# Layer two: three steps of neighbourhood attention placed between the output gate's projection tiles

## The chip, the cores and the metric

One core of a Trainium2 chip runs the kernel; the other cores are idle. The metric is the device time of one execution in microseconds, the median of several runs. The engines are named as in the profile: PE (TensorE, matrix products), DVE (VectorE), ACT (ScalarE), POOL (GpSimd), SP (SyncE, which here issues the DMAs).

## The reference, cut to what matters

A two-layer diffusion backbone over 512 latent tokens (a grid of 8 rows by 64 columns) and 256 context tokens, width 1024, all in float32. Each layer normalises and modulates its input, multiplies it by one wide input matrix, and splits the result into three groups of heads:

```
q_c, kv_c, k_pe, nq, nk, nv, dn = split_in(h @ w_in[l])
mla_o = multi-head latent attention (4 heads, up-projections, softmax over context + latent)
na_o  = neighbourhood attention     (4 heads of 64; 16 columns around each query, plus context)
dn_o  = gated DeltaNet              (4 heads of 128, two directions, chunks; output gate silu(z))
x = x + gate * (concat(mla_o, na_o, dn_o) @ w_out[l])
x = x + gate * swiglu(...)
```

In layer two the context stream is no longer updated, so only the 512 latent tokens are queries there. The three groups of heads don't depend on one another until the output projection. `z`, the DeltaNet's output gate, is one of the slices of the input projection: 512 columns, four tiles of 128.

## The kernel before

Every matrix product on the large weights is done in three passes: weight and activation are each split into a rounded part (`h`) and a remainder (`l`), and `gemm` adds hh, hl and lh. A weight tile is loaded by SP (`wr`), rounded by ACT (`wh`, line 216), and its remainder taken by POOL (`wl`, line 217; a few on DVE).

The code writes one program order per engine, mostly by hand; a planner (the tile framework's scheduler, with a simulated timeline) then fixes the issue order of each engine before the run, and may issue an instruction ahead of earlier ones if its buffers are free. On the chip each engine issues in that fixed order.

The part of a layer that matters here, in program order:

1. *Projections* of keys, values and queries of DeltaNet, with their convolutions; then those of neighbourhood attention (`do_nk`, `do_nq`, `do_nav`). On the side DVE inverts 32x32 blocks (`base_inverse`).
2. *Tail* (lines 979 to 990). `inverse(0, ...)` builds the 128x128 inverses of two chunks from the blocks. Then a string of letters, one for each layer, gives the order of what is left: `k` is `do_kv` (latent keys and values, with a normalisation), `q` is `do_ql` (the two query tiles of latent attention), `z` is `do_z` (the next of four gate tiles: projection into one of two PSUM banks of 512 columns, tanh on ACT at line 794, product on DVE at line 795, store). When the tail is over, the projections' buffers and PSUM banks are released; the DeltaNet's working buffers are claimed on their place.
3. *Neighbourhood attention beside DeltaNet* (lines 1109 to 1112). `attention()` is a generator; each `next(na)` is one step: one of four blocks of 128 queries for one pair of heads, so eight steps in layer two. A step does, for each of two heads, scores on PE (`s_na`, twelve small matmuls for both heads, two PSUM banks), row maxima with the bias added on DVE (lines 870 to 876), two exponentials on ACT (877, 878), the denominator and the scaling on DVE (882 to 884), four transposes on PE (`tp_na`, line 889) and a copy of them (`pt`, line 891, ACT for the first head and DVE for the second); then sixteen small matmuls with the values (`o_na`) and a copy. Only the last step of a pair issues a DMA.
   Before each step `beside` takes as many items from the DeltaNet list `dn` as the list `DNS` says. The items are scans of one chunk in one direction (`scan(d, x)`: state times keys `ks`, product with the inverse `yp`, state update `sp`, and where there is output `qs` and `oa`), the second and third `inverse`, and a release of banks.
4. *Latent attention* (lines 1119 to 1233), with the rest of the list, and then the output projection, which needs all three.

A scan can only start when the DeltaNet's buffers are there, that is after the last gate tile. The second `inverse` begins with four mask products on POOL (line 945) and transposes on DVE.

```
for i in TAIL[l]:
    tail[i]()
...
def beside(ada, sb):
    for _ in range(next(dn_n, 16)):
        next(dn, lambda: 0)()
...
while True:
    beside(ada, sn)
    if next(na, None) is None:
        break
```

Of the kernel before, what the change touches and what calls it, by code (L numbers as in the profile page):

```python
# [34 lines left out]
BN = dict(S=2, T=3)  # L35
BM = dict(S=3, T=3)
ADA = ([2] * 12, [])
DNS = ([1, 0, 0] + [1] * 4 + [0] + [1] * 12, [0, 0, 2, 1, 1, 2, 1, 1, 2, 3] + [2] * 11)
ADA_T = "T"
EB = dict(e=5)  # L40
BO = {512: 3, 256: 2}
# [1 line left out]
PRE0, LATE = True, ()  # L43
ROW = lambda S, V: S.copy
HLP = ([(k, 1) for k in range(8)], [], [(k, 1) for k in (0, 2, 4, 6, 7)], [])
TAIL = ["zzzzkq", "kzzqzz"]
INV = ((4, 3), (4, 3))
WV = ((6,), (23,))
MR = 2
# [313 lines left out]
def layer(tc, nc, a, l, es_x, xT, env, nx):  # L363
# [426 lines left out]
    def do_z(h):  # L790
        n = nT
        th, z = ctmp("thz"), ctmp2("z")
        for cols, acc in proj(TILE_Z + h, need_ctx):
            tanh = S.activation(out=th[:, cols], in_=acc, func=AF.Tanh, scale=0.5)
            stt(out=z[:, cols], in0=th[:, cols], scalar=1.0, in1=acc, op0=ALU.add, op1=ALU.mult)
        if h == 3:
            e.preload(tanh)
        nc.sync.dma_start(out=d_z[:, 0:n // P, h], in_=z[:, :n].rearrange("p (c d) -> p c d", d=P))
# [44 lines left out]
    def open_na():  # L843
        nonlocal sn
        sn = pool(es_w, f"sb_na{l}", side=B_)
# [135 lines left out]
    inverse(0, sb_i, att_bank)  # L981
    if "n" in TAIL[l]:
        open_na()
    z = iter(range(4))
    tail = dict(k=do_kv, q=do_ql, z=lambda: do_z(next(z)), n=lambda: next(na))
    for i in TAIL[l]:
        tail[i]()
    es_i.close()
    es_h.close()
    es_p.close()  # L990
    if "n" not in TAIL[l]:
        open_na()
# [80 lines left out]
    def finish(c, tok, o):  # L1073
# [13 lines left out]
        for h in range(4):  # L1087
# [6 lines left out]
               S_(0, 4), S_(1, 5), S_(0, 5), S_(1, 4), S_(0, 3), S_(1, 2)])  # L1094
    dn_n, ada_n = iter(DNS[l]), iter(range(3 * KD))

# [370 lines left out]
```

## Time and profile before

| | us |
|---|---|
| median of 3 runs | 2146.63 |
| the three runs | 2128.88, 2146.63, 2149.4 |
| the profiled execution, its own time | 2147.42 |
| its span in the profile | 2145.6 |
| PE busy | 2008.8 (94%) |
| DVE busy | 1176.9 (55%) |
| ACT busy | 714.1 (33%) |
| POOL busy | 758.7 (35%) |

The profile is of one execution. Times in it count from the start of its span. The clock that was granted to PE is given as a share of full speed; it has two levels, 1.2 and 2.4 GHz, so 0.50 means that all of a stretch ran at the lower one. A busy PE is not PE at its peak, since its matmuls overlap. Idle time of an engine is put down to what ended it.

### The profile page before, as it was taken

The page shows a single profiled execution, that of the slowest core. Times are in us where ns is not written, and L with a number is a line of the kernel's source. Part 1 is how long each engine was busy: PE and PEld are TensorE (multiplying, and loading weights), DVE is VectorE, ACT ScalarE, POOL GpSimd, SP SyncE. Part 2 cuts the span into 40 slices and gives each one's busy share as a digit, 9 for nine tenths or more (in the row PEclk, how much of TensorE's full clock was granted, in tenths as well). Part 3 has the DMA queues.
Part 4 walks back from the last instruction along what each step waited for, and adds up shares of the span by engine and source line. Part 5 has one row for each costly group of instructions (what it writes and reads, how often), then busy time and mean ns, then how long its engine had stood idle before and what let it go on. Part 6 is the DMA issues. An engine that isn't in the chain of part 4 may idle for free. (4 is left out here: it accounts for less than half of the span.)

```text
span 2145.6 us, 32031 instructions
## 1 busy us (share of the span) xinstructions
PE 2008.8 (94%) x12770; PEld 1699.3 (79%) x12770; DVE 1176.9 (55%) x2045; ACT 714.1 (33%) x1385; POOL 758.7 (35%) x540
## 2 busy tenths in 40 slices
PE   6899998998998999999999998889899889999998
PEld 4788787887787888888888876777688678888887
DVE  4888814768656447347343458882559654222123
ACT  5333323335444121121122344324334443222233
POOL 3465233113323222232323445623202252444444
PEclk9999998999999999999999999999679999999999
DMA  7324253542322435244342512424222232332332
GB/s 278 80 79 147 80 157 100 176 155 77 102 71 79 130 118 164 92 130 158 107 128 70 155 34 71 151 73 134 74 67 87 67 105 67 93 95 94 102 96 91
DMA packets 119309, 232.56 MB, mean 108 GB/s; under 512 B 30516, under 2 KB 55988, under 8 KB 119032
## 3 DMA queue, kind: packets, MB, share of 16 engines
q1 hardware_dynamic: 119160, 230.51, 34.2%
q8 instruction: 101, 1.65, 0.3%
q14 instruction: 48, 0.39, 0.1%
HBM read 199.46 MB, written 31.01 MB: 107 GB/s over the span
## 5 line engine op out<-in xcount | busy, mean ns | idle before, releaser
L217 POOL TENSOR_TENSOR wl<-wr,wh 128x1024 fp32r<-128x1024 f32 (+2 forms) x188 | 440.4, 2343 | 829.3 <-ACT wh L216 810.8
L216 ACT CAST wh<-wr 128x1024 fp32r<-128x1024 f32 (+2 forms) x190 | 193.5, 1019 | 717.9 <-PE acc_gu L104 289.2
L104 PE MATMUL acc_gu<-fh,wh 128*128 128x512 f32 (+1 forms) x1024 | 358.8, 353 | 9.6 <-ACT fh L304 8.7
L104 PE MATMUL acc_gu<-fl,wh 128*128 128x512 f32 (+1 forms) x1024 | 360.7, 353 | 4.1 <-DVE fl L305 4.1
L104 PE MATMUL acc_gu<-fh,wl 128*128 128x512 f32 (+1 forms) x1024 | 359.9, 352 | 0.0
L104 PE MATMUL acc_in<-hh,wh 128*128 128x512 f32 (+1 forms) x640 | 229.0, 362 | 16.9 <-ACT xp L491 6.2
L104 PE MATMUL acc_in<-hl,wh 128*128 128x512 f32 (+1 forms) x640 | 228.6, 358 | 3.0 <-DVE hl L305 2.0
L104 PE MATMUL acc_in<-hh,wl 128*128 128x512 f32 (+1 forms) x640 | 225.3, 356 | 2.1 <-POOL wl L217 2.0
L104 PEld LDWEIGHTS acc_gu<-fh,wh 128*128 128x128 f32 x1024 | 194.0, 190 | 37.2 <-ACT fh L304 11.0
L1348 DVE TENSOR_TENSOR av<-acc_gu,av 128x768 f32<-128x768 f32 (+1 forms) x44 | 36.3, 825 | 337.7 <-PE acc_gu L104 329.7
L104 PEld LDWEIGHTS acc_gu<-fl,wh 128*128 128x128 f32 x1024 | 195.0, 190 | 30.5 <-DVE fl L305 4.3
L104 PEld LDWEIGHTS acc_gu<-fh,wl 128*128 128x128 f32 x1024 | 194.8, 190 | 26.2
L104 PEld LDWEIGHTS acc_in<-hh,wh 128*128 128x128 f32 x640 | 125.1, 196 | 43.3 <-issue 8.1
L104 PE MATMUL acc_d<-al,wh 128*128 128x512 f32 (+1 forms) x444 | 157.2, 354 | 0.0
L104 PE MATMUL acc_d<-ah,wh 128*128 128x512 f32 (+1 forms) x444 | 157.2, 354 | 0.0
L104 PE MATMUL acc_d<-ah,wl 128*128 128x512 f32 (+1 forms) x444 | 156.1, 354 | 0.0
L254 DVE CUSTOM_DVE_ANT_0 junk<-wada,scb 128x1024 f32<-128x1024 f32 x112 | 144.1, 1286 | 7.9 <-DMA wada<-w_adaT 5.2
L104 PEld LDWEIGHTS acc_in<-hl,wh 128*128 128x128 f32 x640 | 125.7, 196 | 24.8 <-DVE hl L305 4.6
L104 PEld LDWEIGHTS acc_in<-hh,wl 128*128 128x128 f32 x640 | 124.8, 196 | 21.1 <-POOL wl L217 3.4
L1366 DVE SCALAR_TENSOR_TENSOR xT<-acc_d,mod,xT 128x512 f32<-128x512 f32 (+1 forms) x76 | 46.5, 634 | 155.4 <-PE acc_d L104 155.4
L501 DVE SCALAR_TENSOR_TENSOR cy<-xp,cw,cy 128x770 f32<-128x770 f32 (+1 forms) x96 | 118.9, 1239 | 22.5 <-ACT cy L499 20.4
L1352 DVE TENSOR_TENSOR al<-av,ah 128x768 fp32r<-128x768 f32 (+1 forms) x44 | 100.4, 2282 | 35.1 <-ACT ah L1351 35.1
(390 smaller groups left out, 3906.2 us busy)
## 6 DMA issues: line engine op xcount, KB each, us to landing
wr<-w_gu SPq DMA_DIRECT2D x88, 512.0 KB, 3.5
wada<-w_adaT SPq DMA_DIRECT2D x56, 512.0 KB, 3.3
wr<-w_in SPq DMA_DIRECT2D x48, 512.0 KB, 3.5
wr<-w_dn SPq DMA_DIRECT2D x32, 448.0 KB, 3.3
wada<-w_ada SPq DMA_DIRECT2D x24, 512.0 KB, 3.4
wada<-w_ada SPq DMA_DIRECT2D x8, 1024.0 KB, 8.3
wr<-w_dn SPq DMA_DIRECT2D x16, 512.0 KB, 3.5
xT<-xT SPq DMA_DIRECT2D x16, 384.0 KB, 5.3
```

Of the source, the lines that this page charges most:

```text
L104: nc.tensor.matmul(out, lhsT, rhs, start=start, stop=stop)
L216: S.copy(out=hi[:, sl], in_=raw[:, sl])
L217: eng.tensor_tensor(out=lo[:, sl], in0=raw[:, sl], in1=hi[:, sl].bitcast(F32), op=ALU.subtract)
L254: V.tensor_tensor_reduce(out=junk, in0=w, in1=scb[:, s], scale=1.0, scalar=0.0, op0=ALU.mult, op1=ALU.add, accum_out=mod[l][:, part, j, s: ...
L501: stt(out=y[:, :wid], in0=xp[:, j:j + wid], scalar=w_(j), in1=y[:, :wid], op0=ALU.mult, op1=ALU.add)
L1348: tt(out=av[:, :nT], in0=accs[1][:, :nT], in1=av[:, :nT], op=ALU.mult)
L1352: after.append(tt(out=l_[:, :nT], in0=av[:, :nT], in1=h_[:, :nT].bitcast(F32), op=ALU.subtract))
L1366: stt(out=xT[:, m, st_], in0=acc, scalar=mod[l][:, 5, m, s:s + 1], in1=xT[:, m, st_], op0=ALU.mult, op1=ALU.add)
```

## The change

Layer two's tail gets the letter `n`, one step of neighbourhood attention, three times, and its order is changed; layer two's list of DeltaNet items for each step is shortened by the three steps that are gone from the later loop (the buffers of the steps are then claimed before the tail instead of behind it).

```
-DNS = ([1, 0, 0] + [1] * 4 + [0] + [1] * 12, [0, 0, 2, 1, 1, 2, 1, 1, 2, 3] + [2] * 11)
+DNS = ([1, 0, 0] + [1] * 4 + [0] + [1] * 12, [2, 2, 2, 1, 1, 2, 3] + [2] * 11)
...
-TAIL = ["zzzzkq", "kzzqzz"]
+TAIL = ["zzzzkq", "kznqznznz"]
```

Before, layer two's order is k, z, z, q, z, z and then eight steps with 0, 0, 2, 1, 1, 2, 1, 1 items ahead of them and 2 behind the last. After, it is k, z, step 0, q, z, step 1, z, step 2, z and then five steps with 2, 2, 2, 1, 1 items ahead of them and 2 behind the last. In both, 10 items of the list are done when the loop ends. Line 982 opens the steps' buffers ahead of the tail when the string has an `n`.

## Rows read from the trace of the kernel before

**Rows 1.** The page, part 2: granted clock of PE in 40 equal slices

```profile
PEclk9999998999999999999999999999679999999999
```

**Rows 2.** Windows of layer two: span, busy time (instructions) by engine, clock, DMA

```profile
1443.00:1507.00 64.00, 58.54 (x440) 47.35 (x439) 15.83 (x37) 26.87 (x45) 22.45 (x12) 0.95 0.44 126
1507.00:1526.70 19.70, 9.92 (x101) 8.21 (x99) 17.34 (x32) 6.56 (x17) 12.15 (x8) 0.83 0.41 135
1526.70:1578.00 51.30, 51.30 (x342) 43.58 (x338) 21.98 (x66) 13.48 (x45) 3.12 (x3) 0.50 0.13 42
1578.00:1608.00 30.00, 30.00 (x403) 26.13 (x403) 19.89 (x50) 10.52 (x32) 2.69 (x4) 1.00 0.21 66
1624.00:1668.00 44.00, 39.36 (x320) 33.96 (x320) 40.06 (x92) 20.80 (x68) 11.04 (x15) 1.00 0.23 68
```

The five engines stand in the order PE, weight loads of PE, DVE, ACT, POOL.

**Rows 3.** Timeline of PE behind the last gate tile: start, duration, what, [idle before]

```profile
1510.31 1.09 PE L104 MATMUL o_na<-pt,nav 128*64 128x128 f32 x16 [2.34 <-ACT pt L891]
...
1515.40 0.63 PE L889 MATMUL tp_na<-cst,pr 128*128 128x128 f32 x4 [2.21 <-DVE pr L884]
1520.09 1.12 PE L889 MATMUL tp_na<-cst,pr 128*128 128x128 f32 x4 [4.07 <-DVE pr L884]
1521.00 1.92 PE L104 MATMUL yp<-vp,Y 128*128 128x128 f32 x8
```

**Rows 4.** Timeline of DVE: the add early and late, and a scaling

```profile
1515.18 2.30 DVE L882 TENSOR_TENSOR st<-st 128x1 f32<-128x1 f32 x1
...
1540.59 0.16 DVE L882 TENSOR_TENSOR st<-st 128x1 f32<-128x1 f32 x1 [1.59 <-ACT pr L878]
...
1543.23 0.49 DVE L884 TENSOR_SCALAR pr<-pr,st 128x512 f32<-128x512 f32 x1
```

**Rows 5.** Groups of DVE from 1507 to 1608: busy us, mean ns | idle before

```profile
L884 DVE TENSOR_SCALAR pr<-pr,st 128x512 f32<-128x512 f32 x14 | 12.0, 857 | 0.4
...
L882 DVE TENSOR_TENSOR st<-st 128x1 f32<-128x1 f32 x14 | 5.5, 395 | 3.6 <-ACT pr L878 3.4
```

**Rows 6.** Timeline of POOL: mask products of the second inverse

```profile
1510.30 9.45 POOL L945 TENSOR_TENSOR Y<-strips,cst 128x1024 f32<-128x1024 f32 x4
```

**Rows 7.** Windows of 2 us, where the clock falls

```profile
1466.00:1468.00 2.00, 2.00 (x8) 1.58 (x8) 1.38 (x4) 0.99 (x2) 1.66 (x1) 0.50 0.92 309
...
1516.00:1518.00 2.00, 0.03 (x1) 0.00 (x0) 1.93 (x3) 0.59 (x1) 2.00 (x2) 0.62 0.61 224
...
1526.00:1528.00 2.00, 2.00 (x21) 1.77 (x17) 1.42 (x5) 2.00 (x9) 0.00 (x0) 0.68 0.04 8
```

**Rows 8.** Timeline of PE: one group of state updates at either clock

```profile
1542.60 2.07 PE L104 MATMUL sp<-w,kt 128*128 128x128 f32 x8
...
1585.84 1.16 PE L104 MATMUL sp<-w,kt 128*128 128x128 f32 x8
```

**Rows 9.** The chain that ended last: start, duration, what

```profile
1573.31 2.00 PE ks L104 x8
1575.31 1.71 PE qs L104 x8
...
1585.00 0.91 PE s_na L104 x6
...
1597.72 0.59 PE tp_na L889 x4
```

**Rows 10.** Timeline of PE: gaps in the tail

```profile
1461.57 0.50 PE L104 MATMUL acc_in<-hh,wh 128*128 128x512 f32 x1 [1.62 <-ACT wh L216]
...
1465.38 0.58 PE L104 MATMUL s_na<-nkh,nqh 64*128 64x256 f32 x1 [1.88 <-ACT pr L878]
```

**Rows 11.** Timeline of ACT: the first gate tile's tanh among exponentials

```profile
1462.49 1.28 ACT L794 ACT_TABLE_LOAD   x1
1463.79 0.60 ACT L794 ACTIVATE thz<-acc_in 128x512 f32<-128x512 f32 x1
1464.28 0.50 ACT L877 ACTIVATE pr<-pr,st 128x256 f32<-128x256 f32 x1
```

## The prediction

> **What bounds the kernel now.** I read the page first: TensorE (PE) is busy 94% of the span, and the row of granted clocks [rows 1] is 9 almost everywhere but for one dip, "67", in the slices from 1502 to 1609 us. That is layer two's neighbourhood attention, the stage that the change touches. So I cut this part into stretches [rows 2]. In the tail stage (1443 to 1507: key/value tile, four gate tiles, query tiles, first block inverse) PE is busy 58.54 of 64 us at a clock of 0.95. Then 1507 to 1526.7: PE busy 9.92 of 19.70, VectorE (DVE) 17.34. Then 1526.7 to 1578: PE busy all 51.30 us, but at 0.50 of its clock. Then 1578 to 1608: PE again busy throughout, at 1.00. The chain of waits agrees: it runs over DVE in the second stretch and over PE in the third and fourth.
>
> Two losses stand there. The first is idle PE after the last gate tile. The next transposes of probabilities wait for the softmax: 2.34, 2.21 and 4.07 us [rows 3], 9.8 of the 19.70 us in all [rows 2]. Two reasons show. The first two attention steps have nothing beside them (zero DeltaNet items each), so one softmax chain is all there is to do; and DVE is slow just then: a one-column add takes 2.30 us where another takes 0.16 [rows 4], and fourteen scalings, 0.49 each when nothing hinders, take 12.0 [rows 4, 5], beside GpSimd's four mask products for the second inverse, 9.45 us from 1510.30 [rows 6]. The second loss follows from the first: the granted clock falls to its lower level at 1516 to 1518 (mean 0.62 there), right in the longest gap, comes back once (0.83 is the mean of the whole stretch), falls again at 1526 to 1528 (0.68) [rows 7], and stays at 0.50 until 1578 [rows 2]. At 0.5 the same eight matmuls take 2.07 us instead of 1.16 [rows 8]; the 51.30 us would be about 25.7 at full clock.
>
> The Trainium skill (TensorE: Matmul & The Clock Gate, HAM oscillation) says that gaps between bursts of matmuls throttle the array, and that sustained activity releases it. The trace agrees with the first half: the fall sits in the 4.07 us gap. It does not bear out the second as far as busy time goes: 51.30 of 51.30 us busy left the clock at 0.50.
>
> **The change part by part.** *What moves.* Steps 0 to 2 of eight go ahead of the second, third and fourth gate tile (step 0 behind the first one and before the query tiles). Of the DeltaNet list, the ten items that stood before the stage's end still stand there; from step 4 on the order is the same as before. What changes is that the first two scans now come before step 3 instead of step 2, and nothing of the steps 0, 1 and 2 stands between the last gate tile and them. Layer one is untouched.
>
> *TensorE.* A step at full clock is two score groups of 0.91 us, two groups of transposes of 0.59 [rows 9] and the values' product of 1.09 [rows 3]: 4.1 us. Scores already run ahead as far as two score banks let them (step 0's before 1443, step 1's in the tail), so what enters the tail is three steps' transposes and products, 6.8 us, step 2's scores and, running ahead in turn, step 3's, 3.6 us: some 10.5. They leave the stage behind. The work is not less; what can be won is idle time and clock.
>
> *Tail.* Now it loses 5.5 us idle [rows 2], of which 1.62 and 1.88 stand where step 0 will be ready [rows 10], and about 3 us from a half-clock piece around 1466 [rows 7] behind those gaps. Bounds: 6.5 us won if the step fills them, 0 if the planner leaves them, and a loss if new gaps come (the rival below); I take 3 won, half of it.
>
> *ScalarE.* Tanh of the gates and exponentials of the softmax now alternate. After the table load for tanh at 1462.49 an exponential runs at 1464.28 with none between [rows 11], so I cost alternation at nothing. The cover for the rest is the slack: ScalarE is busy 26.87 and DVE 15.83 of the tail's 64 us [rows 2]; all of DVE's work from 1507 to 1608 is 59 us (the three stretches of [rows 2]) with eight steps and ten DeltaNet items in it, so three steps bring well under a third, some 14 us as an estimate, which fits. Were that slack gone, the gate's evacuation would be late and hold one of the two projection banks.
>
> *Queues.* Steps 0 to 2 issue no DMA (the output goes out after step 3 of a pair) and nothing on GpSimd, so neither SP's nor GpSimd's queue gets anything; the weights' loads keep their order. On PE the steps are queued past the projections, on ScalarE past their weight casts.
>
> *After the last gate tile.* The loads of the first scan start when that tile's buffers are free, but its product runs only at 1521.00 [rows 3], behind both transposes of step 1. With the scans first it can run 4 to 5 us after the tile, and step 3's softmax can be ready by then, as step 0's was. So of the 9.8 us idle I leave 3: 6.8 won. Bounds: 9.8, and 0 if the mask products starve DVE in the same way, which the trace cannot exclude: they still start there.
>
> *Clock.* From 1507 to 1608 PE has about 8 + 25.7 + 30 = 64 us of full-clock work, 53.5 after the move. If the clock holds, 25.7 us and some 1.6 of the short dip are won. I leave one short dip, 3.3 us: 24. But then DVE binds more. Its work until 1578 is 17.3 + 22.0 us, some 8.4 of it excess of the slow instructions (12.0 - 14 x 0.49 for the scalings, 5.5 - 14 x 0.16 for the adds [rows 4, 5]); less that and some 9.5 for what leaves (the 14 without what already ran ahead), 21.5 against 23 us of PE work. The nearest stretch with both so loaded is 1624 to 1668: DVE 40.06 of 44, PE 39.36, that is 89%, at clock 1.00 [rows 2]. By it 53.5 us of work take 60.1: 6.6 lost. If only the first 23 us suffer it is 3; I take 6.6, since the mask products come on top.
>
> **Sum:** 3 + 6.8 + 24 - 6.6 = 27 us won. The profiled execution took 2147.42 us (span 2145.6 and 1.8 around it), 0.8 over the median of the three runs, 2146.63: so about **2120 us**. The three runs reach from 2128.88 to 2149.4; one 18 us faster would fit a clock that came back earlier, but no trace shows it.
>
> **The rivals.** *The clock falls again and stays.* For it: GpSimd's 9.45 us of masks follow the last gate tile in any order, and DVE instructions with operands in SBUF stall beside them [rows 4, 6]; once low, the clock stayed low over 51 us of mixed small matmuls. Against: denser work right there. In the trace it rose with the first pair of state products that stand side by side (2.00 and 1.71 us from 1573.31 [rows 9]), those of the scan that follows the second inverse; of the changed order some 23 us of full-clock work lie ahead of that, 46 at half instead of the 32 that I allow. Gain 27 - 14: 2134 us. The Trainium skill (SBUF — State Buffer, Who interferes with whom) speaks for this: GpSimd and a DVE instruction with two SBUF operands exclude each other on a shared port, and the later one waits in full. The 2.30 us add agrees with it.
>
> *Nothing is given back.* The planner reorders across steps already (step 1's scores run in the tail), so the issue order may hardly change, or the idle time moves to the scans' chain of matrix product, scaling and state update. Then 2147, give or take 5.
>
> *Slower: the steps stop the projections.* ScalarE and DVE issue in order. If a copy of transposed probabilities is queued ahead of a gate tile's tanh, and its transpose stands on PE behind a projection, the tile's bank stays held and PE waits out the softmax. Price: the waits of a bare step, 2.34 + 2.21 us or up to 4.07 + 2.34 [rows 3], times three, 14 to 19 us, with the low clock later as now: some 2162 us. It decides where such a wait in the tail is over about 3 us a step with no gain behind. Against it: the tail's slack and the two banks.
>
> **How the numbers follow.** Held clock 0.50 (2110 to 2130), low clock again 0.27 (2128 to 2143), nothing 0.11 (2142 to 2152), slower 0.12 (2155 to 2170). 1% is about what a measurement of this kernel can tell from no change; it is 21.5 us, a bound at 2125. Faster: three quarters of the first case and a tenth of the second, 0.40. Slower: 0.13. Within 1%: 0.47. The range: from 2106 (all idle time and no DVE loss) to 2147, which holds the first two cases and half of the third.
>
> **What would show it.** Right: in the profile after, exponentials and transposes of steps 0 to 2 between the gate tiles; the first scan's product within some 5 us of the last gate tile; the clock row without the "67"; the stage after the gate tiles about 60 us instead of 101. The tail longer by about 8 us, not 20. Wrong: a fall of the clock within 10 us of the last gate tile that lasts over 20; gaps of PE over 2 us between gate tiles that end with a transposed copy or a gate's evacuation; or a later stage that takes back what this one wins, since latent attention behind it is the DVE-loaded stretch.

## The result and the profile after

The changed kernel takes 2121.74 us, the median of 7 runs (2119.09 to 2125.45); the kernel before, run beside it, 2147.81 us (7 runs). The ratio is 0.9889, 95% interval 0.986 to 0.9917: 26 us, a little over 1%. The runs of the kernel before spread over the whole study from 2128 to 2162 us, and their mean granted clock goes with the time: at 2128 to 2135 us it is 0.965 to 0.971, near 2147 us 0.958 to 0.962, from 2159 us up 0.952 to 0.955.

The profiled execution of the changed kernel took 2125.45 us (span 2123.6). Its page, part 2, the granted clock in 40 equal slices; the "67" of [rows 1] is gone:

```profile
PEclk9999998999999999999999999999999999999999
```

Windows of the changed kernel, to set beside [rows 2]: the tail; from the end of the last gate tile to the fall of the clock; the low piece; the rest of neighbourhood attention.

```profile
1448.00:1519.30 71.30, 65.62 (x487) 52.30 (x485) 23.81 (x65) 32.52 (x65) 22.65 (x12) 0.93 0.41 116
1519.30:1532.30 13.00, 8.86 (x115) 7.34 (x114) 10.81 (x22) 5.46 (x14) 11.79 (x8) 1.00 0.58 193
1532.30:1539.10 6.80, 6.62 (x45) 6.11 (x45) 2.95 (x12) 2.24 (x6) 1.04 (x1) 0.50 0.14 39
1539.10:1583.70 44.60, 44.60 (x606) 38.87 (x605) 29.71 (x83) 16.60 (x52) 4.94 (x6) 1.00 0.27 75
```

The stage behind the gate tiles is 64.4 us long (1519.3 to 1583.7) where it was 99.2 (1507.0 to the end of the last `o_na` at 1606.2). 6.8 us of it run at half clock; before it was 58.0, in windows of 1 us from 1516.5 to 1523.3 and from 1526.7 to 1577.9. From 1539.1 on PE does not wait at all, with DVE busy 29.71 of 44.60 us.

The timeline of PE in the changed kernel, against [rows 3]:

```profile
1504.19 1.09 PE L889 MATMUL tp_na<-cst,pr 128*128 128x128 f32 x8
...
1510.41 1.09 PE L104 MATMUL o_na<-pt,nav 128*64 128x128 f32 x16
1511.44 0.66 PE L889 MATMUL tp_na<-cst,pr 128*128 128x128 f32 x4
...
1518.93 0.39 PE L104 MATMUL acc_in<-hh,wl 128*128 128x512 f32 x1
1519.25 1.09 PE L104 MATMUL o_na<-pt,nav 128*64 128x128 f32 x14
...
1525.39 0.38 PE L104 MATMUL s_na<-nkh,nqh 64*128 64x256 f32 x1 [1.51 <-ACT pr L878]
...
1526.30 1.16 PE L104 MATMUL yp<-vp,Y 128*128 128x128 f32 x8
...
1532.48 2.08 PE L104 MATMUL sp<-w,kt 128*128 128x128 f32 x8 [2.81 <-DVE w L1035]
...
1535.49 1.97 PE L889 MATMUL tp_na<-cst,pr 128*128 128x128 f32 x8
1537.25 1.91 PE L104 MATMUL yp<-vp,Y 128*128 128x128 f32 x8
```

Step 0 from its transposes on, the transposes of step 1 and the scores of step 2 stand between the gate tiles; step 1's last fourteen products and step 2 from its transposes on run behind the last one. The three waits for softmax of [rows 3] are gone. What is left is 1.51 and 2.81 us. The second wait is the old mechanism at a new victim, as DVE and GpSimd show (timelines of the changed kernel):

```profile
1507.65 0.48 DVE L884 TENSOR_SCALAR pr<-pr,st 128x512 f32<-128x512 f32 x1
...
1515.69 0.48 DVE L884 TENSOR_SCALAR pr<-pr,st 128x512 f32<-128x512 f32 x1
...
1527.91 1.62 DVE L882 TENSOR_TENSOR st<-st 128x1 f32<-128x1 f32 x1
1529.45 0.41 DVE L870 TENSOR_REDUCE st<-s_na 128x1 f32<-128x256 f32 x1
1529.78 2.04 DVE L882 TENSOR_TENSOR st<-st 128x1 f32<-128x1 f32 x1
1531.75 0.68 DVE L1035 TENSOR_TENSOR w<-yp,scal 128x512 f32<-128x512 f32 x1
```

```profile
1522.54 9.27 POOL L945 TENSOR_TENSOR Y<-strips,cst 128x1024 f32<-128x1024 f32 x4
```

The scalings of steps 0 and 1 now run before GpSimd's mask products, at 0.48 us. In the kernel before, those of step 1 stood beside them (timeline of DVE there; two more of the slow instructions behind [rows 5]):

```profile
1512.91 2.35 DVE L884 TENSOR_SCALAR pr<-pr,st 128x512 f32<-128x512 f32 x1
...
1517.71 2.33 DVE L884 TENSOR_SCALAR pr<-pr,st 128x512 f32<-128x512 f32 x1
```

In the changed kernel the scalings have escaped. Two adds still fall beside the mask products (1.62 and 2.04 us), and this time the scaling `w` of the first scan is queued behind. Between the two adds the row maximum, which reads PSUM, takes its usual 0.41 us. The groups of DVE from 1519.3 to 1583.7 say what is left of [rows 5]: the scalings cost nothing extra any more, the adds some 3.3 us.

```profile
L882 DVE TENSOR_TENSOR st<-st 128x1 f32<-128x1 f32 x10 | 4.9, 490 | 0.2
L884 DVE TENSOR_SCALAR pr<-pr,st 128x512 f32<-128x512 f32 x10 | 4.9, 498 | 0.1
```

The gaps of the tail [rows 10] stayed as they were, 1.70 for 1.62 and 1.87 for 1.88 us:

```profile
1467.03 0.50 PE L104 MATMUL acc_in<-hh,wh 128*128 128x512 f32 x1 [1.70 <-ACT wh L216]
...
1470.83 0.58 PE L104 MATMUL s_na<-nkh,nqh 64*128 64x256 f32 x1 [1.87 <-ACT pr L878]
```

### The profile page after: what moved, and what is told of

Same layout as the page of the kernel before. It is cut to its first block, busy times and chain, and to the rows that moved or that the text cites. A ratio compares the mean times of both kernels' runs of the same rounds, so it can differ in the third digit from the quotient of the medians.

```text
span 2123.6 us, 32023 instructions
## 1 busy us (share of the span) xinstructions
PE 1990.2 (94%) x12770; PEld 1684.4 (79%) x12770; DVE 1172.3 (55%) x2045; ACT 714.3 (34%) x1385; POOL 758.7 (36%) x540
```

## The experiments

The theory to test: DVE's divisions beside GpSimd's mask products leave gaps on PE; the gaps pull the clock down; the clock is the larger part of the loss; the steps win because they put the first softmaxes ahead of the masks. The rivals: the list of scans, the query tiles' place, the mere number of steps, or a clock that falls whenever the stage of small products begins. All times are medians; "before" was 2147.3 us beside the first four kernels, 2146.73 beside the next four, 2140.78 beside the ninth and tenth and 2146.95 beside the last two. Stretches at half clock are read from windows of 1 us.

**1. The list alone.**

```diff
-DNS = (..., [0, 0, 2, 1, 1, 2, 1, 1, 2, 3] + [2] * 11)
+DNS = (..., [2, 0, 0, 1, 1, 2, 1, 1, 2, 3] + [2] * 11)
```

> The kernel before, with nothing but its DeltaNet list changed so that the first two scans stand ahead of step 0 and none of the eight steps moves (2, 0, 0, 1, 1, 2, 1, 1, 2, 3). Theory (the gain is the clock that no longer stays low, because the moved steps and what runs ahead of them leave less idle time behind the last gate tile): the list alone moves hardly an instruction, since the planner goes by readiness; 2147 +- 5 us, PE at 0.50 for about 50 us as before. Rival A (the scans that come first are the gain): 2135 us or less, the first scan's product within 5 us of the last gate tile.

2143.12 us, ratio 0.9994 (0.995 to 1.0037). The half clock is where it was, 1516.3 to 1523.2 and 1526.6 to 1577.8. The list hardly reaches the chip: by the names that the traces give, all 12770 matmuls of PE stand in the same order in both kernels (the names do not tell the two directions' scans apart, so that these may have changed places). The planner issues by what is ready, as the expectation said. So the list, on the kernel before, gives nothing; what the change wins must come with the tail's letters.

**2. The query tiles alone.**

```diff
-TAIL = ["zzzzkq", "kzzqzz"]
+TAIL = ["zzzzkq", "kzqzzz"]
```

> The kernel before, with nothing but the order of its tail changed: key/value tile, gate, both query tiles, then three gates; no attention step among them. Theory: 2147 +- 5 us, same gaps behind the last gate tile and the same low clock. Rival B (the query tiles' earlier place is what helps, since their normalisation and its two table loads no longer stand late in the tail): 2138 us or less.

2136.78 us, ratio 0.9962 (0.9928 to 0.9995): some 10 us won with no step moved. My theory's 2147 +- 5 fell, and the rival's 2138 or less came, though its reason (the place of the table loads) is not shown by it. Windows of this kernel, behind the last gate tile:

```profile
1509.98:1514.10 4.12, 1.78 (x25) 1.52 (x23) 2.31 (x8) 4.07 (x9) 3.24 (x4) 1.00 0.17 19
1514.10:1541.40 27.30, 22.16 (x180) 18.77 (x176) 18.97 (x38) 6.57 (x23) 9.95 (x6) 0.50 0.29 99
1541.40:1591.00 49.60, 49.60 (x634) 43.24 (x634) 35.77 (x100) 19.95 (x62) 4.78 (x6) 1.00 0.23 68
```

The waits are nearly the old ones (2.34, 1.53 and 3.61 us). What differs is that the clock came back at 1541.4 instead of 1577.9, with the work behind the gaps in another order. So a kernel can win clock without closing gaps; the sixth and the last two experiments go on from here.

**3. The gaps filled.** The kernel before, with idle matmuls (128 by 128 weights, 512 columns) queued behind the last gate tile, which the computation does not need.

```diff
+def fill(tc, nc, bank, l, r, after, n):
+    junk = bank("fill")
+    with tc.issue_after(after.ins):
+        for _ in range(n):
+            mm(nc, junk, l, r)
...
+                    fill(..., {(1, 0): 10, (1, 1): 16}[qt, j]) if ... else 0
                     tp = att_bank("tp_na")
...
+                fill(..., {0: 10, 1: 5}[qt]) if ... else 0
                 o_ = att_bank("o_na")
```

> The kernel before, with 41 idle matmuls (128x128x512, results never read) queued behind the last gate tile in the gaps of steps 0 and 1; no other work is moved. Theory (clock): about 9 us of otherwise idle PE time is filled, the clock does not fall to 0.50 or comes back within 10 us, and 18 to 24 us come back less up to 5 that the filler delays: 2125 to 2135 us. Rival C (the gain is that three steps' waits are hidden behind projections, and the low clock costs little because PE is not the bound there): the filler hides no wait, so 2147 to 2155 us whatever the clock does.

2135.43 us, ratio 0.9981 (0.9949 to 1.0013), just over the theory's end of 2135, with a spread of 2128.69 to 2147.16: not settled by its time. Its profile, of the slowest execution, says why. The filled stretch kept its clock up to 1532.5; a wait of 3.38 us that I had not filled stood open there up to 1532.15, the clock fell right behind it, and stayed at 0.50 up to 1566.6.

**4. The masks off GpSimd.** Layer two's four mask products of the second and third inverse on VectorE; the tail and the list as before.

```diff
-            G.tensor_tensor(out=Y[d], in0=Ys[d]...
+            (V if l and x0 else G).tensor_tensor(out=Y[d], in0=Ys[d]...
```

> The kernel before, with the four mask products of layer two's second and third inverse on VectorE instead of GpSimd (8 in all), no step moved. Theory: the slow instructions behind the last gate tile (2.30 us for 0.16, 2.33 for 0.49) go back to their short times, the gap of 4.07 us falls below 2; if the clock then holds 2122 to 2132 us, if it falls all the same about 2143. Rival C: only the idle time counts, 4 to 6 us less: 2141 to 2144 us with or without the low clock.

2126.98 us, ratio 0.9919 (0.9881 to 0.9957): 20 of the 26 us, without a step moved. The timeline of DVE in this kernel:

```profile
1512.03 0.16 DVE L882 TENSOR_TENSOR st<-st 128x1 f32<-128x1 f32 x1 [1.35 <-ACT pr L878]
...
1512.97 0.16 DVE L882 TENSOR_TENSOR st<-st 128x1 f32<-128x1 f32 x1
1513.37 0.49 DVE L884 TENSOR_SCALAR pr<-pr,st 128x512 f32<-128x512 f32 x1
...
1517.76 4.63 DVE L945 TENSOR_TENSOR Y<-strips,cst 128x1024 f32<-128x1024 f32 x4
```

Every add is back at 0.16 us and every scaling at 0.49, for 4.63 us of masks on DVE in place of 9.45 on GpSimd. (The four mask products that run in a row are two each of the second and the third inverse; the prediction gave all four to the second. The edit moves these four; the "8 in all" of the expectation was a miscount.) The Trainium skill (SBUF — State Buffer, Who interferes with whom) says that a DVE instruction with two inputs in SBUF contends with a GpSimd instruction that reads SBUF, and that one with at most one SBUF input, outside the modes that take two ports, does not. The 0.16 us here and the 0.41 us row maximum above, beside adds of 1.62 to 2.30, agree. The scalings, with one large input, were stretched all the same (2.35 and 2.33 us for 0.49), so the second half holds here only with its exception; that they run in such a mode no run here shows. The two waits for step 1's transposes are gone, 2.33 and 2.52 us before `o_na` stay, and the half clock behind the gate tiles is 3.4 + 3.5 us in place of 58.

**5. Steps and masks together.** The changed kernel with the masks on VectorE.

```diff
-            G.tensor_tensor(out=Y[d], in0=Ys[d]...
+            (V if l and x0 else G).tensor_tensor(out=Y[d], in0=Ys[d]...
```

> The changed kernel, with layer two's four mask products of the first scans taken from GpSimd to VectorE. Theory (what is left of the loss behind the last gate tile is the same mechanism: the changed kernel's slow st sums of 1.62 and 2.04 us beside the mask products, its gap of 2.81 us before the first sp, and the stretch of half clock from 1531.6 to 1538.4 behind it): gap and stretch go, 2.8 + 3.4 us, less some of the four products on VectorE (1.2 us each): 2115 to 2119 us. Rival (moving the steps and moving the masks win the same thing, and nothing of it is left): 2121 to 2125 us.

2121.12 us (4 runs), ratio 0.9878 (0.9816 to 0.994): no difference from the changed kernel, so the rival holds. Moving the steps and moving the masks win the same thing. The wait before the first `sp` shrank only from 2.81 to 1.89 us, and the low piece grew, 10.2 us from 1526.4.

**6. The steps with the old query order.** This and the ninth and tenth diffs are against the changed kernel.

```diff
-TAIL = ["zzzzkq", "kznqznznz"]
+TAIL = ["zzzzkq", "kznzqnznz"]
```

> The changed kernel, with the query tiles back behind the second gate tile as in the kernel before, and the three steps left in the tail (k z n z q n z n z). Theory (the steps are what fills the gaps behind the last gate tile, and the query tiles' place matters only where no step fills them): 2118 to 2126 us. Rival (the 10 us that the query tiles' place won by itself are part of the 26): 2129 to 2134 us.

2120.84 us, ratio 0.991 (0.9871 to 0.9949): by the median the query tiles' place is worth nothing where steps stand between the tiles. The 10 us of the second experiment are not a separate part of the 26. Three of its ten executions, however, took 2133.28 to 2135.48 us at a mean clock of 0.962 to 0.963, where the changed kernel's seven lie within 2119.09 to 2125.45; whether the early place keeps such executions away was not tested, and none of the three was profiled. The early place even has a price, which the last section shows: a short fall of the clock in the tail, which this kernel lacks.

**7. The last gap filled too.** The diff is against the third experiment.

```diff
-                fill(..., {0: 10, 1: 5}[qt]) if ... else 0
+                fill(..., {0: 10, 1: 19}[qt]) if ... else 0
```

> The kernel before with idle matmuls again, 10, 10 and 16 as in the fill before and 19 in place of 5 ahead of the second step's output product, so that the wait of 3.38 us that was still open at 1528.8 us is filled as well; the idle matmuls are work that the computation does not need. No wait is taken away: all that can be won is clock. Theory (the clock fell at that open wait, and cost about 17 us from 1532 to 1566): the half clock behind the gate tiles is 8 us long at the most, and the time 2120 to 2130 us. Rival (the clock falls anyway when the stage of small products begins): 2133 to 2142 us, with 30 us or more at half clock behind 1530 us.

2130.03 us, ratio 0.9919 (0.989 to 0.9949), at the theory's upper end. Windows of this kernel behind the last gate tile:

```profile
1511.30:1535.50 24.20, 21.06 (x132) 16.34 (x130) 19.31 (x38) 8.56 (x24) 12.32 (x8) 1.00 0.32 102
1535.50:1590.70 55.20, 54.94 (x741) 48.33 (x741) 37.77 (x108) 19.75 (x65) 6.02 (x7) 1.00 0.23 70
```

No half clock at all: the 58 us of it are gone, and nothing else has been won, since the softmax chain is as long as before (step 1's first transposes start 8.3 us behind the last gate tile in the kernel before and 8.4 here) and the steps are where they were. So the clock alone is worth 17 us by the medians; the stage is 79.4 us long in place of 99.2. And the stage of small products does not bring the clock down by itself. That the gaps do is not quite shown: the idle matmuls close the waits and put full-array work in their place, and this experiment cannot tell the one from the other.

**8. Query order and masks.**

```diff
-TAIL = ["zzzzkq", "kzzqzz"]
+TAIL = ["zzzzkq", "kzqzzz"]
-            G.tensor_tensor(out=Y[d], in0=Ys[d]...
+            (V if l and x0 else G).tensor_tensor(out=Y[d], in0=Ys[d]...
```

> The kernel before with the query tiles ahead of the second gate tile, and layer two's mask products on VectorE; no step is moved. Theory (both win by the same gaps and the same clock, so the two gains do not add; the 2.3 us before the first output product and the 2.5 us before the second stay): 2122 to 2130 us, as with the masks alone. Rival (two separate gains of 10 and 20 us): 2114 to 2118 us.

2132.5 us, ratio 0.9923 (0.9895 to 0.9951), just over the theory's end of 2130 and far from the rival's: the two gains do not add. Beside the masks alone it is 5 us longer, with two low pieces (6.8 us from 1520.6, 6.9 from 1530.8).

**9. One step.**

```diff
-DNS = (..., [2, 2, 2, 1, 1, 2, 3] + [2] * 11)
+DNS = (..., [0, 2, 1, 1, 2, 1, 1, 2, 3] + [2] * 11)
...
-TAIL = ["zzzzkq", "kznqznznz"]
+TAIL = ["zzzzkq", "kzzqznz"]
```

> The changed kernel with one step in the tail in place of three (k z z q z n z), the query tiles back behind the second gate tile, the list of scans as in the kernel before less its first number. Theory (each step in the tail takes one gap away from behind the last gate tile; the first step takes the 2.34 us before its output product, and the steps behind it still wait for divisions held up by the mask products on GpSimd, so that the clock still falls): 2130 to 2144 us, with L882 or L884 slowed to over 2 us and 15 us or more at half clock behind the gate tiles. Rival (any step in the tail is enough, since it brings the whole chain of steps forward): 2119 to 2126 us.

2120.9 us, ratio 0.9908 (0.988 to 0.9935): as good as three by its time, and my theory's 2130 to 2144 fell. (Against the 2140.78 us of the kernel before that ran beside it, it wins 20 us, not 26; the two ratios' intervals overlap.) Windows of this kernel, then its DVE and PE:

```profile
1510.84:1521.00 10.16, 7.16 (x81) 5.91 (x80) 9.09 (x22) 5.15 (x13) 9.31 (x7) 1.00 0.69 220
1521.00:1527.80 6.80, 4.30 (x36) 3.80 (x33) 6.11 (x17) 2.30 (x8) 2.67 (x3) 0.50 0.11 40
1527.80:1579.30 51.50, 51.50 (x684) 44.65 (x683) 35.07 (x96) 18.87 (x59) 5.91 (x7) 1.00 0.24 73
```

```profile
1508.56 0.49 DVE L884 TENSOR_SCALAR pr<-pr,st 128x512 f32<-128x512 f32 x1
...
1519.01 2.04 DVE L882 TENSOR_TENSOR st<-st 128x1 f32<-128x1 f32 x1
...
1521.43 2.58 DVE L884 TENSOR_SCALAR pr<-pr,st 128x512 f32<-128x512 f32 x2
```

```profile
1523.76 1.94 PE L889 MATMUL tp_na<-cst,pr 128*128 128x128 f32 x8 [2.50 <-DVE pr L884]
```

The stalled divisions are there, as I expected, and so is a wait of 2.50 us with a fall of the clock. What I had wrong is the count and the aftermath. One step ahead brings the softmax of step 1 forward as well (its scalings end at 1509.05, the masks start at 1514.06), so only one wait for a stalled division is left of two; and the clock is back after 6.8 us.

**10. Four steps.**

```diff
-DNS = (..., [2, 2, 2, 1, 1, 2, 3] + [2] * 11)
+DNS = (..., [2, 2, 2, 1, 2, 3] + [2] * 11)
...
-TAIL = ["zzzzkq", "kznqznznz"]
+TAIL = ["zzzzkq", "knznqznznz"]
```

> The changed kernel with a fourth step in the tail (k n z n q z n z n z, the list one number shorter). Theory (the gaps are filled with three steps; a fourth takes some 2.5 us of TensorE out of the stage behind and puts it under the gate tiles, where the tail grows by as much, and leaves the scans with less to stand between them): 2119 to 2126 us, no difference from three steps. Rival (the work under the gate tiles goes into the gaps of the tail, 1.9 and 1.6 us, that three steps leave open): 2113 to 2118 us. A third outcome, the scans laid bare too early: 2128 us or more, with gaps before sp and yp.

2118.83 us (2112.53 to 2123.76), ratio 0.9905 (0.9871 to 0.9939): not to be told from three or from one. PE is idle 1.6 us from the last gate tile to 1545, in place of the changed kernel's 4.3; the low clock is 10.2 us there and 10.3 more from 1574.0. No version here beats the changed kernel by more than the measurement can tell.

This trace also speaks against gaps as the whole cause. PE's timeline where the clock first falls, at 1516.0, shows only short waits:

```profile
1513.56 1.16 PE L104 MATMUL yp<-vp,Y 128*128 128x128 f32 x8 [0.31 <-DMA vp<-d_v]
...
1515.64 0.41 PE L104 MATMUL pp<-mix,LP 32*32 32x32 f32 x8 [0.92 <-DVE st L876]
1516.25 1.96 PE L104 MATMUL pp<-mix,LP 32*32 32x32 f32 x40 [0.20 <-DMA LP<-d_LP]
```

Behind 1.6 us of idle time in all the clock was down for 10.2 us, longer than the 6.8 us that followed the changed kernel's waits of 1.51 and 2.81 us. So the length of the waits alone does not set the loss.

**11 and 12. Big and small tiles behind the open gaps.** If gaps alone set the loss, what runs behind them should not matter. The kernel before, its gaps left open, with 24 idle matmuls behind the last one (they close only the short wait of 1.17 us that comes next, in both versions): first on the full array, then (the last two lines of the diff) on 32 rows by 32 columns of it, with the same 512 columns moving.

```diff
+                    fill(..., 24) if l and not pair and (qt, j) == (2, 0) else 0
                     tp = att_bank("tp_na")
...
-            mm(nc, junk, l, r)
+            mm(nc, junk[0:32], l[0:32, 0:32], r[0:32])
```

> The kernel before with its three gaps left open, and 24 idle matmuls of the full array (128 rows by 128 columns of weights, 512 columns moving) behind the last of them: 17 between the second step's first and last output products, 7 behind the first sp. The idle matmuls are work that the computation does not need, some 24 x 0.24 = 6 us at full clock. Theory, as the run with one step leaves it (the gaps pull the clock down for a short dip, and how long it stays down is set by what runs next: the stage's many small tiles kept it low for 51 us, big tiles bring it back): the half clock behind the gate tiles is 15 us in all or less instead of 57, some 20 us are won and 6 paid: 2130 to 2138 us. Rival (the gaps alone set the loss, whatever runs behind them): 2150 to 2158 us, the clock down for 45 us or more.

2137.63 us, ratio 0.9949 (0.9932 to 0.9967). Windows of it:

```profile
1511.90:1525.60 13.70, 8.41 (x30) 6.73 (x31) 13.40 (x23) 0.68 (x2) 7.75 (x5) 0.50 0.43 155
1525.60:1587.30 61.70, 61.70 (x782) 53.25 (x782) 40.13 (x116) 23.36 (x75) 5.81 (x7) 1.00 0.21 60
```

> The same 24 idle matmuls at the same places, on 32 rows by 32 columns of the array in place of 128 by 128; the same 512 columns move, so the engine is busy for as long. Theory (small tiles do not bring the clock back): down for 45 us or more as in the kernel before, and 24 x 0.24 to 0.43 us longer than it: 2152 to 2160 us. Rival (any work without a gap brings it back, so that the size of the tile does not matter): 2130 to 2138 us, like the burst of full tiles.

2142.86 us, ratio 0.9969 (0.9952 to 0.9987). Windows of it:

```profile
1512.00:1559.80 47.80, 42.42 (x198) 29.80 (x196) 23.13 (x56) 8.63 (x27) 9.64 (x7) 0.50 0.18 60
1559.80:1606.70 46.90, 46.90 (x640) 41.24 (x639) 32.16 (x86) 15.95 (x51) 4.82 (x6) 1.00 0.23 66
```

The two kernels are alike up to the burst (waits of 2.34, 1.68 and 3.61 us in the one, 2.34, 1.77 and 3.62 in the other, the clock down at 1511.9 and 1512.0). Within the big burst the clock came back, at 1525.6, and stayed for the rest of the stage, though the small products follow as ever. The first seventeen small tiles ran through at half clock in 7.46 us (the big ones took 5.34), and the clock was back only at 1559.8. Idle work of 7.2 us made the kernel 9 us faster.

The time of the twelfth is a miss all the same: 2152 to 2160 was expected. Its profiled execution, 2148.4 us, is the slowest of its ten; five others took 2135.73 to 2140.19 us at a mean clock of 0.962 to 0.965. In those the clock must have been low for a shorter time, and I have no trace of one. So that the clock came back within the burst of big tiles, and stayed, is shown by one trace, and the times of all seven executions (mean clock 0.966 to 0.969) fit it; that it does not come back within the small ones is shown by one trace, and the times say that it is not so in every execution.

## Why the prediction was right

The forecast was 2120 us, the case "held clock". The steps of its sum against the two profiled executions (the changed one reached this stretch 4.9 us later than the one before: step 0's first scores start at 1428.36 instead of 1423.46. The change does not bear on that: PE's order is the same in both up to 1496 us, and the seventh experiment's kernel, which is the one before up to the last gate tile, starts them at 1427.24. It is taken off):

| term | predicted | measured |
|---|---|---|
| tail | +3 | -1.6 |
| idle behind the last gate tile | +6.8 | +5.5 |
| clock | +24 | +23.6 |
| DVE binds more | -6.6 | 0 |
| later stages | 0 | -0.6 |
| sum | 27 | 26.9 |

*Tail.* It ends at 1519.3 instead of 1507.0, less 4.9: 7.3 us longer, close to the 8 that were named. Some 5.7 of it is the work that moved in (two groups of 1.09, the transposes 2 x 0.66, 0.43 of step 1's product and step 2's scores, some 1.8). The rest, 1.6 us, is a loss: the gaps of [rows 10] were not filled, and 3.4 us more ran at half clock, from 1498.2 (the last section has the rows). The step that failed is the guess that the planner would put step 0 into these gaps.

*Idle.* 9.8 us before, 4.3 us after up to 1545. Right, and the 3 us left over were named; the mask products still hold DVE, as the lower bound had allowed.

*Clock.* The prediction lets the half clock follow from the idle time and names the longest gap. That gap, 4.07 us, holds the first fall, which lasted 6.8 us. The second fall, at 1526.7, brought the other 51.2 us, and the only wait between the clock's return at 1523.3 and this fall is one of 1.17 us, which the prediction does not name (timeline of the kernel before):

```profile
1525.48 1.09 PE L104 MATMUL o_na<-pt,nav 128*64 128x128 f32 x14 [1.17 <-DVE pt L891]
```

So the size of the term came out right, but that the second loss follows from the first is borne out by that trace for its small part only; the seventh experiment bears it out for the whole, with the reserve named there. The stage is 34.8 us shorter (99.2 to 64.4). Less the 5.7 us of work that left and the 5.5 of idle, 23.6 remain; the one short dip that I left is there (1532.3 to 1539.1). That this is clock and nothing else is shown from the other side by the seventh experiment, which removes the half clock alone. It puts 17 us on it; I take the smaller figure as the one that is measured by itself, since the 23.6 is what the other terms leave.

*DVE.* The term of -6.6 was wrong. I took the 89% of latent attention over to a stage whose DVE is busy 29.71 of 44.60 us; PE did not wait there once. The two misses, 4.6 us less in the tail and 6.6 more here, nearly cancel, and that the sum is closer than its terms is luck.

*Later.* Latent attention did not take the gain back. A wait of 3.48 us for DVE's `rr`, up to 1609.36, and 6.8 us of half clock from 1607.1 are new, but half clock from 1585 to the last matmul is 13.6 us in both.

*The order.* "The first two scans now come before step 3" was put down to the list. The list does nothing (first experiment). The first scan's product does run ahead of step 3's transposes, 7.0 us behind the last gate tile, where some 5 were named, but because it was ready. And step 2 was said to stand among the gate tiles: it runs behind them.

*The rivals.* "The clock falls again and stays" had the mechanism half right: it does fall again, in the wait that the mask products leave (2.81 us). But it lasted 6.8 us, not 46. The reason given, that it comes back with a pair of state products, was too narrow: in the changed kernel `sp`, eight transposes and `yp`, tiles of 128 by 128 with twenty of 32 by 32 among them, stand ahead of its return at 1539.1, and the eleventh experiment brings it back with idle tiles of that size. "Nothing is given back" and "slower" did not come: no wait over 2 us stands between the gate tiles.

Open: what exactly brings the clock down, beside the waits, and what lets it return. The low stretch behind the gaps was 51.2 us in the kernel before, 27.3, 34.1 and 47.8 in three others of this study, 51.2 again with the list alone and 10.3 or less at a stretch in most of the rest, and the spread of one kernel's runs shows that it varies from run to run. That three steps are needed is refuted, as far as the ninth experiment's time can tell, since one does as much; which of the moved instructions does it was not taken further apart.

## What to carry to other kernels

Where a short idle stretch is followed by a long one at half clock with PE busy throughout, price the clock first: here it was worth some two to four times the idle time before it (17 us of clock for 9.8 us idle by the seventh experiment, 23.6 for 5.5 by the table). Look for the cheapest cause of the gap, which may lie on an engine that is nowhere near busy (four mask products put on another engine won 20 us by themselves, where the steps won 26), and expect cures of the same gap not to add. A change in a list that a planner reads is no change until the issue order shows it.

## What was unexpected of the hardware

The clock also fell where PE never waited. Windows of the changed kernel's tail, and PE's timeline there without the gate tile's products:

```profile
1484.00:1502.00 18.00, 18.00 (x184) 15.00 (x183) 3.80 (x9) 7.81 (x13) 3.12 (x2) 0.91 0.15 52
...
1498.00:1500.00 2.00, 2.00 (x6) 1.51 (x5) 0.00 (x0) 1.97 (x3) 0.00 (x0) 0.54 0.00 0
```

```profile
1492.66 1.90 PE L104 MATMUL pp<-X,LP 64*64 64x64 f32 x32
1494.49 1.91 PE L104 MATMUL yq<-strips,p 32*32 32x32 f32 x64
1496.32 1.05 PE L104 MATMUL ms_q<-cst,sqs 128*128 128x2 f32 x8
```

PE is busy all of 18.00 us from 1484 to 1502. Three groups of small products follow one another up to 1497.4, and at 1498.2 the clock is at half for 3.4 us; then, with the gate tile's products of 128 by 128 by 512 running, it is back. The kernels with the query tiles behind the first gate tile (the second, fifth and eighth experiment) show the same fall of 3.4 us, at 1493.6, 1492.3 and 1500.1; those with the tiles behind the second one do not. Nor does the one with four steps, though the same three groups follow one another there, from 1482.7 to 1487.4; so they do not always bring a fall. The Trainium skill (TensorE: Matmul & The Clock Gate, HAM oscillation — how this bites in real kernels) puts such falls down to waits between bursts of matmuls. Most of the falls behind the last gate tile agree, since they come in a wait of over 1 us or within some 2 us of one. Three do not fit well, those at 1516.0 and 1574.0 with four steps and at 1530.8 in the eighth experiment, which have only waits under 1 us there (0.92, 0.68 and 0.46). The fall in the tail has none at all: there the Trainium skill and the trace differ, and the measurement decides.

Idle work can pay: 24 matmuls of the full array, 7.2 us of them behind open gaps, made the kernel 9 us faster. And four multiplications of 128 by 1024 took 9.45 us on GpSimd and 4.63 on DVE, those on GpSimd stretching a one-column add on DVE from 0.16 to 2.30 us.
